# A two-layer hybrid decoder trunk on one core: the feed-forward weight buffers dealt out anew, and the scheduler's times taken from another simulation

## The chip, the core and the metric

The kernel runs on one core of a Trainium2 chip. A core has a matrix engine (TensorE, "PE" in the profile, with its weight loads as "PEld"), a vector engine (VectorE, "DVE"), an engine for activation functions and copies (ScalarE, "ACT"), a general one (GpSimd, "POOL"), and SyncE ("SP"), which here only issues DMA transfers. Each engine works through a queue of its own in order, and the queues wait for each other by semaphores. The metric is device microseconds for one execution of the program; lower is better. One execution was also taken by the hardware profiler, and its page and trace are what the prediction argues from.

## The reference

The trunk holds 16 learned meta tokens and 512 real tokens of width 1024. Layer 0 mixes by multi-scale retention (4 heads), layer 1 by a gated delta rule with a short convolution (8 heads). Behind each mixer stands a SwiGLU feed-forward block of hidden width 2816, and each of the four steps is added to the residual stream. Cut to what matters:

```python
def swiglu(h, w_gate, w_up, w_down):
    return (jax.nn.silu(h @ w_gate) * (h @ w_up)) @ w_down

for i in range(DEPTH):
    hn = rmsnorm(h, mix_norm_w[i])
    mix = retention(hn, ...) if i == 0 else gated_deltanet(hn, ...)
    h = h + mix
    h = h + swiglu(rmsnorm(h, ffn_norm_w[i]), ffn_w_gate[i], ffn_w_up[i], ffn_w_down[i])
return rmsnorm(h, final_norm_w)[:, CHUNK:, :]
```

All is float32. The kernel gets that accuracy by splitting each operand into a high and a low part in a reduced format and adding three products (`mm3`, line 400): high x high, high x low and low x high.

## The kernel before, in words

Tokens lie along the columns (528 = 16 + 512), features along the 128 partitions in 8 blocks. The stages follow each other: retention (`retention`), its output projection, feed-forward block 0 (`ffn0`), DeltaNet (`deltanet`), feed-forward block 1 (`ffn1`).

**Weights.** Every weight tile is 128 x 1024 float32 (512 KB). SyncE loads it into a raw buffer. ScalarE casts it to the high part `whi`, VectorE subtracts to get the low part `wlo` (`split_w` and `split`, line 396; in `load_w`, line 159, the same two steps are lines 170 and 171). `whi` and `wlo` have three buffers each. The raw buffers `wraw` are four, shared by the whole kernel (`raw_w`, line 174, with `RAW = 4`).

**Feed-forward, first half** (`ffn_hidden`). The 22 blocks of hidden features are worked off as 11 *quads*: a quad is two rows of blocks for gate and up, in two halves of the features, so four weight tiles called 11, 21, 22 and 12. `ffn_quad` (line 334) loads them in that order, one DMA each on SyncE's queue (line 339). The first two quads are multiplied plainly. The other nine go through `strassen` (line 342), a scheme with seven products instead of eight. Its seven products read, in order: tile 11; 21 + 22 (line 374); that plus 11 (line 377); that plus 12 (line 380); 11 + 21 (line 385, written over tile 21); tile 12; tile 22. The running sum is the one buffer `wsum`. Each product is split like a weight tile and takes 24 matmuls on TensorE (8 weight blocks of 128 x 128, three partial products each). The hidden activations leave PSUM through lines 364 and 368 and go through the SiLU and the product (lines 955 to 961).

Of a quad's four tiles, 11 and 12 stand in `wraw`, and 21 and 22 in a tag `sraw` with two buffers, in a pool that lives only as long as the first half of a block. After the first half, the down projection loads its weights into `wraw` by `load_w` (line 164 issues).

**Retention.** Its projections use a like scheme of seven products (`quad`, line 275), fed by `wraw` alone (line 257 issues, `quad_part` adds at line 264). As each product ends, `taken` copies or adds PSUM away (lines 287 to 304); line 291 is the copy after the first product, line 293 that after the second. The target of these copies is `at`, the memory that the rotary step (`rope`, line 520, VectorE operations of line 530 and splits) uses as scratch for the head before. PSUM pairs `g` are two, single banks `m` four.

**DeltaNet.** After keys, gates and values, a scan over four chunks for each head runs as a chain of small matmuls and evacuations (`dn_scan`); the projections of the following heads are interleaved with it on TensorE by hand: generators with fixed delays in "ticks", one tick for every group of matmuls (`spawn`, `tick`, and the constants `HOP`, `VALUES`, `ATTEND` and others).

**What sets the order.** The program is written in one order, which is the priority. When the `TileContext` closes, a scheduler plays the program on a simulated machine. At each simulated moment an engine takes, of the instructions whose inputs and buffers are ready there, the one that stands first in the program. The order that comes out is the order of that engine's queue on the chip, fixed from then on. Buffers of a tag are handed out in the same play: an instruction that needs a buffer becomes ready when an earlier holder has given it back.

Of the kernel before, what the change touches and what calls it, by code (L numbers as in the profile page):

```python
# [14 lines left out]
P = 128  # L15
# [35 lines left out]
class Hybrid:  # L51
# [282 lines left out]
    def ffn_quad(self, src, sp):  # L334

        raw = {}
        for i, n in enumerate(("11", "21", "22", "12")):
            raw[n] = self.raw_w() if n[0] == "1" else self.t(sp, [P, 1024], "sraw", bufs=2)
            self.nc.sync.dma_start(raw[n], src[i])
        return raw  # L340

# [1433 lines left out]
```

## Time and profile before

| | us |
|---|---|
| three runs | 1739.11, 1740.63, 1741.30 |
| median | 1740.63 |
| profiled execution: time | 1740.59 |
| profiled execution: span from first to last instruction | 1738.8 |
| mean granted TensorE clock in it | 0.990 |

How to read the profile: "busy" is the time in which an engine had an instruction in work. TensorE's matmuls are pipelined, so the durations of neighbours overlap and their starts give the pace. A wait is the idle time of an engine in front of an instruction, with the instruction that released it. The chain of waits goes back from the last instruction to what released each step. "PEclk" is the clock that TensorE was granted, as a share of full speed. A line such as L398 can be that of a helper, so the tile's name tells which use it is: `wlo<-wsum` is the low part of a running sum.

By stretches of the span, retention lies at about 10 to 372 us, its output projection at 372 to 463, feed-forward block 0 at 463 to 834, DeltaNet at 834 to 1395, and feed-forward block 1 from there to the end.

### The profile page before, as it was taken

To read this page: it belongs to the slowest core of one execution; us is meant where nothing else is said; L and a number is where in the kernel's file an instruction comes from. 1 tells how busy PE (TensorE), PEld (TensorE's weight loads), DVE (VectorE), ACT (ScalarE), POOL (GpSimd) and SP (SyncE) were. 2 spreads that over 40 slices of the span, in tenths; PEclk is the share of its full clock that TensorE was granted. 3 is DMA by queue.
4 is the path that set the end of the run, shared out by engine and by line. 5 is a ranking of instruction groups with operands and counts; after the bars stand their busy time and mean duration, and the time that the engine had idled before them with its cause. 6 is when DMAs were issued, how large, how long until landed. Compare 5 with 4: busy or idle time off the path is not lost.

```text
span 1738.8 us, 30404 instructions
## 1 busy us (share of the span) xinstructions
PE 1696.0 (98%) x12455; PEld 1577.0 (91%) x12455; DVE 1209.5 (70%) x1830; ACT 854.8 (49%) x1524; POOL 75.8 (4%) x130
## 2 busy tenths in 40 slices
PE   9999999899999999999999999999999999999997
PEld 9998989899999999999999978797977889999886
DVE  7868787873497777533688777685858797777322
ACT  5554454553354544422565537665656544445322
POOL 1000000000000000000030000010101000000010
PEclk9999999999999999999999999999999999999999
DMA  6333234472313332333264463332322233333321
GB/s 215 134 97 121 86 108 142 139 246 87 110 62 98 113 107 82 100 89 95 81 209 159 132 180 114 120 113 98 113 96 75 86 97 97 98 99 108 97 97 49
DMA packets 84524, 197.72 MB, mean 114 GB/s; under 512 B 19888, under 2 KB 37472, under 8 KB 83104
## 3 DMA queue, kind: packets, MB, share of 16 engines
q1 hardware_dynamic: 77056, 193.13, 34.2%
q10 hardware_dynamic: 6960, 1.84, 0.5%
q8 instruction: 98, 1.61, 0.4%
q0 software_dynamic: 368, 0.80, 0.1%
q14 instruction: 42, 0.34, 0.1%
HBM read 171.41 MB, written 24.33 MB: 113 GB/s over the span
## 4 chain that ended last, share of the span: by engine, by line
PE 72%; DVE 16%; ACT 5%; DMA 4%; issue 3%; POOL 1%; ACTq 0%; SPq 0%; DVEq 0%; POOLq 0%
PE g L407 53%; PE m L407 13%; DVE wlo L398 5%; ACT whi L397 3%; DMA sraw<-in_w_gu_dram 3%; DVE wraw L264 1%; DVE wsum L380 1%; DVE wsum L377 1%; DVE wsum L374 1%; DMA wraw<-in_w_ret_dram 1%; DVE xlo L530 1%; DVE wlo L171 1%; DVE xhi L398 1%; POOL ss L1435 0%; DMA xhi<-d_sg 0%
## 5 line engine op out<-in xcount | busy, mean ns | idle before, releaser
L171 DVE TENSOR_TENSOR wlo<-wraw,whi 128x1024 fp32r<-128x1024 f32 (+1 forms) x140 | 166.4, 1191 | 177.5 <-ACT whi L170 175.4
L170 ACT CAST whi<-wraw 128x1024 fp32r<-128x1024 f32 (+1 forms) x140 | 143.3, 1024 | 261.8 <-PE g L407 141.3
L407 PE MATMUL g<-fht,whi 128*128 128x264 f32 (+1 forms) x864 | 248.2, 287 | 13.2 <-ACT xlo L291 13.0
L407 PE MATMUL g<-xhi,whi 128*128 128x264 f32 (+1 forms) x1024 | 254.3, 313 | 0.1
L407 PE MATMUL g<-xhi,wlo 128*128 128x264 f32 (+1 forms) x1024 | 247.6, 306 | 2.0 <-DVE wlo L171 2.0
L407 PE MATMUL g<-xlo,whi 128*128 128x264 f32 (+1 forms) x1024 | 247.8, 306 | 0.3 <-DVE xlo L461 0.3
L407 PE MATMUL g<-fht,wlo 128*128 128x264 f32 (+1 forms) x864 | 245.6, 284 | 0.9 <-DVE wlo L398 0.8
L407 PE MATMUL g<-flt,whi 128*128 128x264 f32 (+1 forms) x864 | 245.3, 284 | 0.0
L407 PEld LDWEIGHTS g<-fht,whi 128*128 128x128 f32 x864 | 163.0, 189 | 14.0 <-ACT xlo L291 13.6
L407 PEld LDWEIGHTS g<-xhi,whi 128*128 128x128 f32 x1024 | 165.9, 189 | 10.7 <-issue 0.7
L407 PEld LDWEIGHTS g<-xhi,wlo 128*128 128x128 f32 x1024 | 165.9, 189 | 10.6 <-DVE wlo L171 2.2
L407 PEld LDWEIGHTS g<-xlo,whi 128*128 128x128 f32 x1024 | 166.2, 189 | 7.5 <-DVE xlo L461 0.7
L407 PEld LDWEIGHTS g<-fht,wlo 128*128 128x128 f32 x864 | 162.7, 188 | 1.7 <-DVE wlo L398 1.6
L407 PEld LDWEIGHTS g<-flt,whi 128*128 128x128 f32 x864 | 163.2, 189 | 0.0
L397 ACT CAST whi<-wraw 128x1024 fp32r<-128x1024 f32 x107 | 111.9, 1049 | 97.7 <-issue 36.6
L398 DVE TENSOR_TENSOR wlo<-wraw,whi 128x1024 fp32r<-128x1024 f32 x107 | 129.9, 1220 | 25.8 <-ACT whi L397 25.7
L407 PE MATMUL g<-fhb,wlo 128*128 128x264 f32 (+1 forms) x432 | 124.1, 287 | 4.8 <-DVE wlo L398 4.7
L407 PE MATMUL g<-fhb,whi 128*128 128x264 f32 (+1 forms) x432 | 123.2, 285 | 0.0
L407 PE MATMUL g<-flb,whi 128*128 128x264 f32 (+1 forms) x432 | 122.4, 283 | 0.0
L397 ACT CAST whi<-wsum 128x1024 fp32r<-128x1024 f32 x54 | 56.7, 1050 | 79.8 <-DVE wsum L377 46.7
L398 DVE TENSOR_TENSOR wlo<-wsum,whi 128x1024 fp32r<-128x1024 f32 x54 | 66.0, 1222 | 40.4 <-ACT whi L397 40.4
L407 PEld LDWEIGHTS g<-fhb,wlo 128*128 128x128 f32 x432 | 81.2, 188 | 7.5 <-DVE wlo L398 7.4
(454 smaller groups left out, 3955.6 us busy)
## 6 DMA issues: line engine op xcount, KB each, us to landing
wraw<-in_w_ret_dram SPq DMA_DIRECT2D x56, 512.0 KB, 3.4
wraw<-in_w_gu_dram SPq DMA_DIRECT2D x44, 512.0 KB, 3.4
sraw<-in_w_gu_dram SPq DMA_DIRECT2D x44, 512.0 KB, 3.4
wraw<-in_w_d_dram SPq DMA_DIRECT2D x38, 512.0 KB, 3.5
wraw<-in_w_ro_dram SPq DMA_DIRECT2D x16, 512.0 KB, 3.9
wraw<-in_w_dqk_dram SPq DMA_DIRECT2D x16, 512.0 KB, 3.3
wraw<-in_w_dv_dram SPq DMA_DIRECT2D x16, 512.0 KB, 3.6
wraw<-in_w_dg_dram SPq DMA_DIRECT2D x16, 512.0 KB, 3.4
```

The lines of the kernel that those rows point to most:

```text
L170: nc.scalar.copy(hi[:, c], raw[:, c])
L171: nc.vector.tensor_tensor(lo[:, c], raw[:, c], hi[:, c].bitcast(F32), op=ALU.subtract)
L264: self.nc.vector.tensor_tensor(raw[dst], raw[dst], raw[src], op=ALU.add)
L374: nc.vector.tensor_tensor(s, raw["21"], raw["22"], op=ALU.add)
L377: nc.vector.tensor_tensor(s, s, raw["11"], op=ALU.add)
L380: nc.vector.tensor_tensor(s, s, raw["12"], op=ALU.add)
L397: self.nc.scalar.copy(hi, src)
L398: self.nc.vector.tensor_tensor(lo, src, hi.bitcast(F32), op=ALU.subtract)
L407: mm(o, l, r[which], start=first and n == 0, stop=last and n == 2, **kw)
L530: nc.vector.tensor_tensor(o, x, y, op=op)
```

## The change

Two edits. In `ffn_quad` only tile 22 is left in `sraw`; tile 21 joins 11 and 12 in `wraw`. The numbers of buffers stay (four `wraw`, two `sraw`), and so do the loads and their order in the program. And the `TileContext` gets a flag: the scheduler plays the program on another simulated machine, a timeline simulation of the devices, in place of the one that it uses by default. The instructions of the kernel stay the same; the order of each engine's queue may differ anywhere in the program.

```diff
@@ -335,7 +335,7 @@ def ffn_quad
         raw = {}
         for i, n in enumerate(("11", "21", "22", "12")):
-            raw[n] = self.raw_w() if n[0] == "1" else self.t(sp, [P, 1024], "sraw", bufs=2)
+            raw[n] = self.t(sp, [P, 1024], "sraw", bufs=2) if n == "22" else self.raw_w()
             self.nc.sync.dma_start(raw[n], src[i])
         return raw
@@ -1768,7 +1768,7 @@ def kernel
-    with _tile.TileContext(nc) as tc:
+    with _tile.TileContext(nc, schedule_with_timeline_sim=True) as tc:
         hybrid_kernel(tc, args, out)
```

## The prediction, made before the changed kernel was run

> **What bounds the kernel now.** I read the head of the page first, then the list of who waited for whom on TensorE, then the chain of waits, and last the timelines at the places that these named.
>
> ```profile
> span 1738.8 us, 30404 instructions
> PE 1696.0 (98%) x12455; PEld 1577.0 (91%) x12455; DVE 1209.5 (70%) x1830; ACT 854.8 (49%) x1524; POOL 75.8 (4%) x130
> ```
>
> TensorE is busy for 1696.0 of 1738.8 us, and the change touches none of its work. What can be won is the idle rest, 1738.8 - 1696.0 = 42.8 us, and any time at a low clock. What can be lost has no such bound. The waits of the whole span are these (the columns are the sum in us, how many, and the longest):
>
> ```profile
> PE g L407 <- ACT xlo L291: 13.0, 3, 5.1
> PE g L407 <- DVE wlo L398: 5.5, 13, 0.6
> PE g L407 <- DVE wlo L171: 2.3, 2, 2.0
> PE m L1140 <- DVE vs L1133: 2.2, 1, 2.2
> PE m L407 <- ACT rh L397: 2.2, 5, 1.0
> ...
> PE m L1448 <- ACT vs L1436: 1.6, 3, 1.0
> PE g L407 <- ACT oh L397: 1.3, 1, 1.3
> ```
>
> Row one is retention, row two the feed-forward quads, the others DeltaNet. About 9.4 us more are idle in the last stretch, which ends in the final scaling and the stores and which nothing in this change shortens:
>
> ```profile
> 1668.00:1739.00 71.00, 61.57 (x264) 49.17 (x262) 18.12 (x25) 16.26 (x25) 6.33 (x7) 0.95 0.20 67
> ```
>
> (The columns of such a row: stretch, length, busy us of TensorE, its weight loads, VectorE, ScalarE and GpSimd, then the granted clock, the DMA share and GB/s.)
>
> **Part one, the feed-forward buffers.** Before, tiles 11 and 12 of a quad come from the four wraw buffers, and 21 and 22 from the two sraw buffers. So tile 22 of the next quad may not be fetched before the last product of this quad has had its weights split. The chain of waits shows what this does in the second feed-forward layer (start, length, what):
>
> ```profile
> 1470.38 4.33 DMA sraw<-in_w_gu_dram
> ...
> 1474.74 1.23 DVE wsum L374
> ...
> 1479.23 1.14 DVE wsum L377
> ...
> 1485.19 1.24 DVE wlo L398
> ...
> 1486.47 2.79 PE g L407 x21
> ...
> 1491.62 3.72 DMA sraw<-in_w_gu_dram
> ```
>
> The split of tile 22 ends, the load of the next one starts at 1470.38, the sum 21+22 (L374) waits for it until 1474.74, three rounds of add, cast and subtract follow, and TensorE gets the weights of the fourth product late, at 1486.47. The next load starts at 1491.62, so this quad lasts 21.24 us. The pace of TensorE alone is read in a long stretch of the same layer, 14.50 us for 119 matmuls or 0.122 us each; a quad has 7 x 24 = 168 matmuls, so 20.5 us:
>
> ```profile
> 1432.77 14.50 PE g L407 x119
> ```
>
> The loop through the DMA is thus longer than the work, by 0.7 us in this quad. The two layers differ:
>
> ```profile
> 505.00:650.00 145.00, 143.97 (x1174) 143.16 (x1173) 115.77 (x133) 71.14 (x97) 0.00 (x0) 1.00 0.31 95
> 1450.00:1600.00 150.00, 146.97 (x1207) 145.09 (x1206) 117.94 (x139) 72.81 (x103) 0.00 (x0) 1.00 0.31 96
> ```
>
> In about seven quads each, layer 0 (where a half is 264 columns wide) idles 1.0 us and layer 1 (256 columns) 3.0 us. The clock is 1.00 in both, so an idle microsecond costs no more than itself.
>
> After the change 11, 21 and 12 take wraw buffers and 22 alone takes sraw, two deep. Next quad's 11 goes into the fourth wraw buffer, next 21 into that of 11, which is free after the sum of L377 and the one of L385, both in the first half of a quad, and next 22 into the sraw buffer that the quad before gave back. The sum of L377 runs at 1479.23 in the rows above, the load of tile 22 now at 1491.62: next 21 and 22 can be issued from there on, for 22 half a quad or some 11 us earlier than now. Next 12 has the latest release, that of 21 after its split for the fifth product, and is needed only for the fourth product's sum, five products on. A load takes 4.33 us in the row above, so it is covered. The loop is cut, and what is late next is TensorE itself. This is worth the second row of the waits, **5.5 us**; bounds 0 (another wait of the same length stands behind it) and 6.4 us (0.71 us a quad in all nine of layer 1, the mean of six loops between the first and the last of the loads below, (1574.83 - 1449.63) / 6 = 20.87, against 168 x 0.120 = 20.16 by the fastest stretch of this layer). I take 5.5, the row of TensorE itself.
>
> ```profile
> 1429.89 2.88 PE m L407 x24
> ...
> 1449.63 3.76 DMA sraw<-in_w_gu_dram
> ...
> 1574.83 4.39 DMA sraw<-in_w_gu_dram
> ```
>
> The number of loads stays: per layer eleven quads of four. All stay on SyncE's queue in the order 11, 21, 22, 12. A load that waits for a wraw buffer holds up those behind it, and at the end of a layer these are the first down-projection weights:
>
> ```profile
> 669.25 0.33 SPq L164 DMA_DIRECT2D wraw<-in_w_d_dram  x1
> ...
> 681.60 17.56 SPq L164 DMA_DIRECT2D wraw<-in_w_d_dram  x4
> ```
>
> ```profile
> 693.50 1.05 ACT L170 CAST whi<-wraw 128x1024 fp32r<-128x1024 f32 x1
> ```
>
> With three buffers taken by the last quad instead of two, these two move back one release each: the load now at 669.25 becomes the first, the second takes the place of 681.60. The first of them is cast at 693.50, the second some 3 us later, so a load of 4.3 us from 681.60 still fits behind the last quad's products; I put it at nothing, and at 4.3 us at most were that cover gone.
>
> **Part two, the order.** The scheduler emits each engine's instructions as its own simulated machine finds them ready; the flag swaps that machine. No instruction is added or removed, but every queue may come out in another order, and no row of before can show it. I bound it by what order costs now. The worst place is in retention, three times alike (ScalarE, then VectorE, then TensorE; start, length, instruction, idle before and its releaser):
>
> ```profile
> 147.68 1.07 ACT L397 CAST qkhi<-xlo 128x1056 fp32r<-128x1056 f32 x1 [4.89 <-DVE xlo L530]
> ...
> 151.15 0.60 ACT L291 COPY xlo<-g 128x528 f32<-128x528 f32 x1
> ...
> 217.11 1.07 ACT L397 CAST qkhi<-xlo 128x1056 fp32r<-128x1056 f32 x1 [4.89 <-DVE xlo L530]
> ```
>
> ```profile
> 145.22 1.25 DVE L530 TENSOR_TENSOR h<-h,sinr 128x1056 f32<-128x1056 f32 x1
> 146.39 1.25 DVE L530 TENSOR_TENSOR xlo<-xlo 128x1056 f32<-128x1056 f32 x1
> ...
> 148.73 1.22 DVE L264 TENSOR_TENSOR wraw<-wraw,wraw 128x1024 f32<-128x1024 f32 x1
> 149.86 1.25 DVE L398 TENSOR_TENSOR qklo<-xlo,qkhi 128x1056 fp32r<-128x1056 f32 x1
> ```
>
> ```profile
> 151.80 0.59 PE L407 MATMUL g<-fht,whi 128*128 128x264 f32 x1 [3.94 <-ACT xlo L291]
> ```
>
> The copy L291 empties a PSUM tile into the memory that the rotary step uses as scratch, so it must wait for the last reader of that scratch, the subtraction that ends at 151.1. Two VectorE steps stand ahead of that without need: the product of 145.22 (1.17 us until the next start) and the add L264 of 148.73 (1.13 us). A better order gains at most 2.3 us of the 3.94 here, 6.9 us over the three places. Behind the waits the clock is low:
>
> ```profile
> 151.80:160.00 8.20, 8.20 (x31) 6.55 (x32) 5.96 (x10) 3.69 (x4) 0.00 (x0) 0.62 0.11 42
> 221.20:228.00 6.80, 6.76 (x24) 5.30 (x25) 5.10 (x10) 3.10 (x4) 0.00 (x0) 0.62 0.15 56
> 310.80:317.00 6.20, 6.18 (x24) 4.88 (x25) 5.96 (x10) 3.06 (x3) 0.00 (x0) 0.65 0.35 102
> ```
>
> That is 8.20 x 0.38 + 6.80 x 0.38 + 6.20 x 0.35 = 7.9 us, lost on top. Whether a wait cut to 1.6 us would still be followed by it, this row bears on:
>
> ```profile
> 874.56 1.74 PE L1140 MATMUL m<-tri,vs 128*128 128x128 f32 x8 [2.24 <-DVE vs L1133]
> ```
>
> ```profile
> 876.00:878.00 2.00, 2.00 (x11) 1.92 (x10) 1.93 (x3) 0.24 (x2) 0.01 (x1) 0.50 0.64 245
> ```
>
> A wait of only 2.24 us stands just ahead of half clock. The Trainium skill, page "TensorE: Matmul & The Clock Gate", section "Part 1", says that the clock falls to half after at least one idle window of about 3.4 us; by that rule a wait of 1.6 us costs no clock, and this term would reach 14.8 us. The row of 2.24 us speaks against so long a window here.
>
> So the term of order lies between 0 and 6.9 + 7.9 = 14.8 us of gain in retention. Likewise the DeltaNet rows of the waits sum to 2.3 + 2.2 + 2.2 + 1.6 + 1.3 = 9.6 us, the most that order can win there; what it can lose there is the slower rival. I take a third of the retention bound, **4.9 us** (near the row of the wait itself: most of it is a true dependency, and only its VectorE share depends on order), and 0 for DeltaNet, between its 9.6 us and a loss.
>
> Sum: 5.5 + 4.9 = 10.4 us. The profiled execution took 1740.6 us, its span 1738.8 and 1.8 around it, and the median of the runs is the same, 1740.6. Forecast: 1740.6 - 10.4 = **1730.2 us**. Its own range goes from 1740.6 - 5.5 - 14.8 = 1720.3 to 1735.1.
>
> **The rivals.** *The order gains nothing*: the new times rank the instructions as the old did at these places. For it: L291 waits on a real dependency, and the cast ahead of it waits 4.89 us in two of the three places, to the hundredth, so it follows from rules more than from chance. Only the buffers count: 1740.6 - 5.5 = 1735.1 us.
>
> *Given back*: the buffers gain 5.5 us and the new order makes one more wait like that of L291, 3.94 us and 7.9 / 3 = 2.6 us of clock: 1740.6 - 5.5 + 6.5 = 1741.6 us, no change that a measurement can tell.
>
> *Slower: weight casts in front of the DeltaNet scan.* The scan is a serial chain between TensorE and ScalarE, and in the same stage ScalarE casts weights ahead of need (columns: line, engine, shape, count, busy us and mean ns, idle and releaser):
>
> ```profile
> L170 ACT CAST whi<-wraw 128x1024 fp32r<-128x1024 f32 (+1 forms) x140 | 143.3, 1024 | 261.8 <-PE g L407 141.3
> ```
>
> If the new machine finds these casts ready earlier than the evacuations of the scan, each scan step waits for one cast, 1.02 us. A head has four chunks with four ScalarE steps each in its chain; for the last pair no other products are left to fill TensorE, so 16 x 1.02 = 16.4 us show, with two spells of low clock at 2.6 us: 21.6 us, less 5.5. 1740.6 + 16.1 = 1756.7 us. It decides from 6 such casts on (6.1 us against 5.5). For it: the delays in the program that spread this stage are fixed numbers, suited to one order. Against it: scan waits are now only 2.2 and 1.6 us in sum, and VectorE and ScalarE have slack.
>
> **Chances.** Forecast, both parts gain: 0.36. Order gains nothing: 0.20. Given back: 0.15. Slower: 0.29. A measurement of this kernel can tell about 0.2%, 3.5 us, from no change; the first two lie beyond it, so faster 0.56, same 0.15, slower 0.29. The range takes in the rivals on both sides: below, nearly the sum of all gains, 1740.6 - 5.5 - 14.8 - 6 (most of DeltaNet's 9.6) = 1714; above, the slower rival and two more spells of low clock, 1756.7 + 5.2, so 1762.
>
> **What would show it.** Right: no wait of TensorE on L398 in the quads and quads of layer 1 of 20.2 to 20.5 us; the sum L374 no longer waits for a DMA; the waits on L291 under 3 us, with VectorE running the subtraction of the rotary step ahead of the second product. Wrong: L291 at 13 us or more in sum with the quads free (first rival), a wait in a place that has none now (second), or TensorE idle by over 15 us between 870 and 1345 us with casts of L170 ahead of scan evacuations on ScalarE (third). The whole is wrong if the quads still wait: then something other than tile 22's buffer holds the loop.

## The result, and the profile after

| | before | after |
|---|---|---|
| median, us | 1740.97 (4 runs, 1739.11 to 1743.44) | 1797.82 (4 runs, 1793.6 to 1799.72) |
| ratio | | 1.0322, 95% interval 1.030 to 1.0345 |
| profiled execution, us | 1740.59 | 1793.6 |
| its span, us | 1738.8 | 1791.8 |
| mean granted clock | 0.990 | 0.970 |

The change makes the kernel 3.2% slower. The forecast was 1730.2 us, its range ended at 1762. The head of the page after:

```profile
span 1791.8 us, 30421 instructions
PE 1726.1 (96%) x12455; PEld 1604.1 (90%) x12455; DVE 1211.3 (68%) x1830; ACT 858.8 (48%) x1526; POOL 70.4 (4%) x130
```

TensorE runs the same 12455 matmuls; ScalarE has two instructions more, table loads of 1.28 us each (11 against 9), which came with the new order. TensorE's idle time rose from 42.8 to 1791.8 - 1726.1 = 65.7 us, by 22.9. Its busy time rose by 30.1 us, and the same matmuls are busy for longer where the clock is lower: of the 53.0 us more, over half is not waiting but slow work (a row below shows a matmul of 0.28 us that takes 0.41). These are TensorE's waits after (sum, times, longest):

```profile
PE g L407 <- ACT whi L397: 24.9, 5, 9.0
PE m L1412 <- DVE wl L398: 4.6, 7, 1.4
PE m L1448 <- ACT vs L1436: 3.3, 6, 0.9
PE m L407 <- DVE s L1423: 2.9, 7, 0.5
PE m L407 <- DVE rr L1397: 2.8, 6, 0.7
PE m L407 <- ACT rh L397: 1.9, 5, 0.7
PE g L407 <- DVE wlo L398: 1.5, 2, 1.0
```

The 13 waits of the quads on L398 are gone; two remain at the entries of the blocks. The chain of waits shows the quads of layer 1: two pieces of one kind start 20.16 us apart, and the window beside them has no idle time in 160 us:

```profile
1512.55 14.40 PE g L407 x120
...
1532.71 14.40 PE g L407 x120
```

```profile
1500.00:1660.00 160.00, 160.00 (x1325) 159.50 (x1324) 127.24 (x151) 82.80 (x114) 0.00 (x0) 1.00 0.31 103
```

So the buffers do what was expected. The first row of the waits is in part retention's old stalls, now 4.2, 4.2 and 5.8 us (13.0 us in sum before), and in part a new wait of 9.0 us at the entry of the second feed-forward block. Most of the rows below it are new or larger, many and short: they lie in DeltaNet's scan. Its four pairs of heads, from merge to merge and to the end of the scan, first before, then after:

```profile
1043.00:1105.00 62.00, 59.15 (x488) 51.45 (x487) 49.28 (x100) 45.86 (x119) 7.44 (x14) 1.00 0.35 114
1105.00:1191.00 86.00, 85.80 (x615) 71.77 (x614) 60.43 (x110) 54.86 (x127) 5.86 (x14) 1.00 0.35 113
1191.00:1277.00 86.00, 85.58 (x614) 71.76 (x614) 60.04 (x109) 54.11 (x125) 5.70 (x12) 1.00 0.33 105
1277.00:1342.00 65.00, 62.62 (x396) 47.70 (x396) 41.73 (x83) 39.86 (x97) 4.54 (x8) 1.00 0.27 91
```

```profile
1044.00:1122.00 78.00, 70.82 (x482) 57.41 (x481) 49.95 (x98) 47.10 (x119) 5.21 (x14) 0.87 0.29 95
1122.00:1217.00 95.00, 91.09 (x614) 75.95 (x614) 59.81 (x110) 53.41 (x125) 5.78 (x14) 0.95 0.30 96
1217.00:1320.00 103.00, 97.53 (x673) 82.29 (x674) 63.22 (x113) 56.55 (x131) 5.00 (x12) 0.98 0.31 99
1320.00:1387.00 67.00, 59.89 (x318) 45.41 (x312) 38.37 (x78) 36.61 (x91) 4.37 (x8) 0.82 0.19 64
```

Read the columns for length, TensorE's busy time with its matmuls, and the clock: before, 1.00 in every pair; after, 0.82 to 0.98, and the first pair takes 16 us longer for about as many matmuls.

What differs, the timeline of TensorE shows. In the same steps of a pair's chain (L1320, L1376, L1385), before:

```profile
1116.63 0.68 PE L1320 MATMUL m<-z,rr 64*64 64x64 f32 x8
...
1118.84 0.60 PE L1376 MATMUL m<-vs,um 16*16 16x256 f32 x2
...
1120.28 0.60 PE L1376 MATMUL m<-vs,um 16*16 16x256 f32 x2
```

and after:

```profile
1133.80 1.14 PE L1320 MATMUL m<-z,rr 64*64 64x64 f32 x16
1134.88 0.60 PE L1376 MATMUL m<-vs,um 16*16 16x256 f32 x2
...
1139.82 0.60 PE L1376 MATMUL m<-vs,um 16*16 16x256 f32 x2
```

The lines left out are output products of other heads (`g<-oh,whi` and the like), the filler that keeps TensorE at work while the chain goes through ScalarE and VectorE. Before, a step gets some 1 to 2 us of it; after, 4 to 5 us stand between the two steps L1376. The queue as the program has it, for the last pair (a number in brackets is filler in us at the full clock, an estimate from the columns of its matmuls; S, R, W and Wk are the matmuls of the scan on its state, its rows and its weights):

```
before: [1.4] L1314 [0.7] L1314 [1.4] L1320 [0.7] L1320 [1.4] L1376 ... [1.4] L1385 [0.7] S [0.9] S [0.5] S [0.9] S [0.5] R [0.7] R L1412 [0.9] L1412 [0.5] Wk [0.7] W Wk ...
after:  [4.5] L1314 [4.7] L1320 L1376 L1380 [3.8] L1376 [0.7] L1380 [0.5] L1385 [4.0] L1385 [0.9] S [0.2] S [3.3] S R S R L1412 R Wk L1412 W Wk S Wk S W S R S R ...
```

The filler is spent early, in bunches, and a step behind a bunch cannot start before it, since the queue is in order. Then the rest of the scan runs bare. In that part the clock falls; the same matmul in the last pair (TensorE, start, length, in brackets the wait):

```profile
1351.26 0.28 PE L407 MATMUL m<-rh,zl 128*128 128x256 f32 x1
1351.38 0.28 PE L407 MATMUL m<-rl,zh 128*128 128x256 f32 x1
1352.29 0.38 PE L407 MATMUL m<-sh,zh 128*128 128x256 f32 x1 [0.64 <-DVE rr L1397]
...
1353.76 0.33 PE L1412 MATMUL m<-ident,z 128*128 128x128 f32 x1 [0.52 <-DVE wl L398]
...
1357.32 0.41 PE L407 MATMUL m<-sh,zh 128*128 128x256 f32 x1
1357.53 0.41 PE L407 MATMUL m<-sh,zl 128*128 128x256 f32 x1
```

```profile
1355.00:1372.00 17.00, 14.87 (x56) 12.14 (x56) 12.81 (x33) 10.36 (x28) 1.53 (x3) 0.50 0.06 25
```

A matmul follows the one before by 0.12 us at 1351 and by 0.21 us at 1357: two waits of 0.64 and 0.52 us stand between, and then 17 us at half clock, in which TensorE is busy for 14.87. All this is what the two edits did together; what caused it is the matter of the runs.

### The profile page after: what moved, and what is told of

Read it like the earlier page. It is cut to its first block, busy times and chain, and to the rows that moved or that the text cites. A ratio compares the mean times of both kernels' runs of the same rounds, so it can differ in the third digit from the quotient of the medians.

```text
span 1791.8 us, 30421 instructions
## 1 busy us (share of the span) xinstructions
PE 1726.1 (96%) x12455; PEld 1604.1 (90%) x12455; DVE 1211.3 (68%) x1830; ACT 858.8 (48%) x1526; POOL 70.4 (4%) x130
## 4 chain that ended last, share of the span: by engine, by line
PE 87%; DVE 5%; ACT 3%; issue 2%; DMA 2%; POOL 1%; SPq 0%; POOLq 0%; ACTq 0%; DVEq 0%
PE g L407 66%; PE m L407 16%; DMA wraw<-in_w_ret_dram 1%; PE m L504 0%; DVE xlo L530 0%; DMA d_dec<-zl 0%; DVE h L530 0%; DMA z<-d_mp 0%; PE m L618 0%; DVE wlo L171 0%; POOL ss L1435 0%; PE m L491 0%; DVE wlo L398 0%; DMA d_m<-z 0%; PE m L1171 0%
## 5 line engine op out<-in xcount | busy, mean ns | idle before, releaser
L170 ACT CAST whi<-wraw 128x1024 fp32r<-128x1024 f32 (+1 forms) x140 | 143.4, 1025 | 326.6 <-PE g L407 205.5
L407 PE MATMUL g<-xhi,whi 128*128 128x264 f32 (+1 forms) x1024 | 250.4, 308 | 1.2 <-DVE ra L937 0.8
L397 ACT CAST whi<-wraw 128x1024 fp32r<-128x1024 f32 x129 | 134.9, 1051 | 126.1 <-PE g L407 68.3
L398 DVE TENSOR_TENSOR wlo<-wraw,whi 128x1024 fp32r<-128x1024 f32 x129 | 157.2, 1221 | 38.5 <-ACT whi L397 38.0
L407 PE MATMUL g<-fhb,whi 128*128 128x264 f32 (+1 forms) x432 | 124.1, 287 | 14.2 <-ACT whi L397 14.2
L407 PEld LDWEIGHTS g<-fhb,whi 128*128 128x128 f32 x432 | 81.9, 190 | 14.9 <-ACT whi L397 14.8
L398 DVE TENSOR_TENSOR wlo<-wsum,whi 128x1024 fp32r<-128x1024 f32 x54 | 66.2, 1225 | 40.8 <-ACT whi L397 40.8
L407 PEld LDWEIGHTS g<-flb,whi 128*128 128x128 f32 x432 | 81.6, 189 | 0.0
```

Of the source, the lines that this page charges most:

```text
L170: nc.scalar.copy(hi[:, c], raw[:, c])
L397: self.nc.scalar.copy(hi, src)
L398: self.nc.vector.tensor_tensor(lo, src, hi.bitcast(F32), op=ALU.subtract)
L407: mm(o, l, r[which], start=first and n == 0, stop=last and n == 2, **kw)
```

## The experiments

Every kernel was timed in three rounds beside the kernel before, whose medians in the four sets were 1741.58, 1742.6, 1740.84 and 1740.13 us. In the tables a profiled span is cut at two marks: the end of DeltaNet's first convolution pad (L1017), and the end of its last output product taken up (L1510).

| kernel | span | to DeltaNet | DeltaNet | rest |
|---|---|---|---|---|
| before | 1738.8 | 841.7 | 526.5 | 370.6 |
| after | 1791.8 | 843.9 | 572.7 | 375.2 |
| e1_buffers | 1728.4 | 836.9 | 526.5 | 365.0 |
| e2_flag | 1799.7 | 848.7 | 568.8 | 382.2 |

**One edit each.** The buffers alone, with the scheduler's first machine:

```diff
-    with _tile.TileContext(nc, schedule_with_timeline_sim=True) as tc:
+    with _tile.TileContext(nc) as tc:
```

> Only the weight buffers are dealt anew; the scheduler keeps its default machine. If the buffers are worth the waits of TensorE on L398 and nothing else, 1740.6 - 5.5 = 1735 us, and the nine quads of the second feed-forward layer last 20.2 to 20.5 us each. The rival, that the buffers themselves are part of the loss, expects more than 1744 us.

1732.98 us, ratio 0.9956 (0.9939 to 0.9972): 8.6 us faster. And the flag alone, with the buffers as before:

```diff
-            raw[n] = self.t(sp, [P, 1024], "sraw", bufs=2) if n == "22" else self.raw_w()
+            raw[n] = self.raw_w() if n[0] == "1" else self.t(sp, [P, 1024], "sraw", bufs=2)
```

> Only the scheduler's machine is swapped; the buffers stay as before. If the two edits add up, 1797.8 + 5.5 = 1803 us, with the quads of the second feed-forward layer still at 20.9 us. If the loss came from the two together, less than 1765 us.

1801.57 us, ratio 1.0349 (1.0334 to 1.0365). So the whole loss is the new order. Against e1_buffers the kernel after loses 63.4 us of span: 7.0 ahead of DeltaNet, 46.2 in it and 10.2 behind it. Of the 46.2 us in DeltaNet, TensorE is busy for 30.0 (515.7 to 545.7) and idle for 16.2.

**TensorE's queue held.** An order can be tried by itself: a first program is planned with one machine, its queue is read, and in the second program each instruction of that queue is tied to the one ahead of it. The other queues are planned anew by the second machine, around the one that is held, so they too come out in an order that differs from the kernel after. "In DeltaNet" is the code from the start of the scan's generators up to `ffn1`. With `pinned` standing for those ties:

```diff
-    nc = program(True)
+    nc = program(True, pinned(program(False), ("PE",)))   # ties in DeltaNet only
```

> Both edits, but in DeltaNet's scan stage TensorE's queue is put into the order that the default machine gives; all other queues are as the new machine makes them around that. Theory: the new machine puts bursts of 2 to 5 us of other products between two steps of the scan on TensorE's queue, so these run out and the rest of the scan runs bare, at a low clock; then the 46 us that the stage grew by come back, about 1752 us (1748 to 1762), and the last stretch of each pair runs at clock 1.00. Rival: the order on ScalarE and VectorE (casts ahead of the scan's evacuations) holds the scan; then it stays within 10 us of 1797.8.

1774.91 us, ratio 1.0194 (1.0179 to 1.021): 23 us back, between the two expectations. TensorE's waits show what took the place (e3, the two rows of DeltaNet that lead):

```profile
PE m L407 <- DVE rr L1397: 7.6, 10, 1.1
PE m L1290 <- DMA z<-d_mp: 7.1, 2, 3.6
```

TensorE's old queue now stands beside a new order of loads and of VectorE's work, and waits for both. So the theory that TensorE's bunches are all of it fell, and the next four runs divide the rest. First, the DMA queue held as well, ("PE", "SP"):

> Both edits, with TensorE's queue and the queue of the DMAs that SyncE issues held in DeltaNet in the order that the scheduler's first machine gives them. With TensorE's queue alone held, 1774.9 us came out, and its profile shows TensorE waiting 7.1 us for the load of z from d_mp (L1290) between 1040 and 1060 us, with the clock at 0.5 to 0.67 up to 1070 us. Theory A, that what was left there is the DMAs' order against TensorE's: those two waits go, and the 16 us that this kernel lost to the first kernel between the first and the second pair's merge (78.4 us instead of 61.9) go with them: 1759 us (1754 to 1764). Rival B, that what was left comes from the order on VectorE and ScalarE: within 5 us of 1774.9.

1768.33 us, ratio 1.0154 (1.0132 to 1.0175). The wait on z shrank to 4.4 us in one piece, and 6.6 us came back, not 16; the ten waits on L1397 stayed at 7.6 us. Both theories have a share here. Then all five queues held, in DeltaNet:

> Both edits, with the queues of all five engines held in DeltaNet in the order of the first machine, the DMAs' among them; retention, the first feed-forward block and the last block keep the new order. Theory A, that the loss in DeltaNet is a matter of queue order and nothing else: the stage takes what it takes with the buffers alone (first merge to the last output product 325 us), and only the 7 to 8 us before it and the up to 10 us at the entry of the last block are left over 1733 us: 1750 us (1741 to 1756). Rival B, that the order of the queues explains only TensorE's share and the rest comes with the new order from the stages before (transfers and clock): over 1760 us.

1744.6 us, ratio 1.0015 (1.0003 to 1.0028). DeltaNet takes 525.8 us as with the first machine: the loss there is a matter of queue order and of nothing else. Then everything held but TensorE, ("SP", "Activation", "DVE", "Pool"):

> Both edits, with the queues of SyncE's DMAs, ScalarE, VectorE and GpSimd held in DeltaNet in the order of the first machine, and TensorE's queue left to the new one. Theory A, that the bunching of filler products on TensorE's queue is the root: TensorE's queue still has bunches of 2 to 5 us between steps and bare runs of steps, so that little comes back: 1785 to 1800 us. Rival B, that the order on VectorE and ScalarE holds the steps back, and TensorE only follows: 1775 us or less.

1813.63 us, ratio 1.0412 (1.039 to 1.0434): nothing came back, and 16 us went on top, more than either expectation. And the converse, buffers new, first machine, and TensorE's queue alone in the new machine's order:

```diff
+    nc = program(False, pinned(program(True), ("PE",)))   # ties in DeltaNet only
```

> The buffers new and the scheduler's first machine, with TensorE's queue alone held in DeltaNet in the order that the new machine gives it, bunches and bare runs of steps among them. Theory A, that this order of TensorE's queue costs what it costs wherever it stands: 1733.0 us and 25 to 45 us on it, 1758 to 1778 us, with the granted clock of 1000 to 1400 us well under 1. Rival B, that it costs only together with the other queues' new order: under 1745 us.

1792.7 us, ratio 1.0289 (1.0269 to 1.0309): on a kernel of 1733.0 us TensorE's order, with the rest planned around it, costs 60 us, more than expected. The window of its last pair has the same mark as after, low clock with few idle microseconds (e8):

```profile
1327.00:1399.00 72.00, 65.41 (x338) 50.49 (x334) 41.08 (x83) 38.84 (x98) 4.97 (x8) 0.74 0.17 59
```

The lengths of DeltaNet beside each other:

| TensorE's queue | the others | DeltaNet, us | run |
|---|---|---|---|
| old | old | 526.5; 525.8 | e1; e6 |
| old | planned by the second machine around it | 553.4 | e3 |
| old | DMAs old, the rest planned by the second machine around both | 549.5 | e5 |
| new | new | 572.7 | after |
| planned by the second machine around the others | old | 593.4 | e7 |
| new | planned by the first machine around it | 587.7 | e8 |

The traces show which orders these are. By line, tile and shape, the last 2400 matmuls of DeltaNet follow each other in e8 as in the kernel after, and in e3 and e6 as in e1. In e7 TensorE's queue parts from the kernel after at the 85th matmul from the end: it is a third order, and e7 does not price the new one.

TensorE's new order is thus enough for the loss: with the rest planned around it by the first machine it costs 61 us, where the whole loss in DeltaNet is 46 (e8). It is not all of it in the kernel after: with TensorE's old queue 19 of the 46 us came back, and the other queues as the second machine plans them around it cost 27 (e3). The costs do not add up; that the queues of one plan fit each other would explain it. That it is the bunches in TensorE's new order that cost the time is read off its timeline; no run moved the filler and left the rest of that order alone.

**The entry of the last block.** Behind DeltaNet the kernels after and e6 lose 9 to 10 us. In e6 TensorE's wait there is much the same as after (9.0 us there):

```profile
PE g L407 <- ACT whi L397: 8.5, 1, 8.5
```

The timeline of ScalarE in the kernel after says where it begins: the row factor `rb` of the norm waits 4.54 us for TensorE's small matmul L500, which stands behind other matmuls in the queue.

```profile
1433.88 0.17 ACT L508 COPY rb<-m 128x16 f32<-128x16 f32 x1 [4.54 <-PE m L500]
```

So all queues were held from DeltaNet to the end of the program:

> Both edits, with the queues of all five engines held in the first machine's order from DeltaNet to the end of the program; only retention and the first feed-forward block keep the new order. Theory A, that the wait of 8.5 us at the entry of the last block is a matter of order too (the steps of its row norm stand behind other products in TensorE's queue): the 9 to 10 us there go as well, and what stays over 1733 us is the 6 us lost before DeltaNet: 1735 to 1740 us against 1744.6 with DeltaNet alone held. Rival B, that this wait comes from the time at which DeltaNet ends or from the transfers: within 3 us of 1744.6.

1736.33 us, ratio 0.9976 (0.9965 to 0.9986): the rest takes 365.0 us as in e1_buffers, so this wait is order too; that it begins with L500 is read off the timeline. Of 63.4 us some 8 us ahead of DeltaNet are left (845.2 us to the mark against 836.9); no run held the queues there.

**Retention's three stalls.** The prediction's gain by order sat here. First the scratch that it named, taken away from the rotation, on e1_buffers:

```diff
-            return self.spawn(self.rope(qk, ct, at, cosr, sinr), ROPED)
+            return self.spawn(self.rope(qk, ct, bt, cosr, sinr), ROPED)
```

> The buffers dealt anew, the default machine, and the rotary step of heads 1 to 3 takes the other half of the scratch memory (bt in place of at), so that the copy after the first product of the next quad (L291) no longer waits for the rotary step. If that copy waits for the scratch and not for a place in ScalarE's queue, the 13.0 us of waits and 7.9 us of low clock go: 1735.1 - 20.9 = 1714 us. If ScalarE's in-order queue holds it (the cast of the rotary result stands ahead of it and waits for VectorE), it gains under 7 us: 1728 to 1735 us.

1730.39 us, ratio 0.994 (0.9925 to 0.9954): 2.6 us under e1_buffers, with runs of the two that overlap. The number is that of the second expectation, but its reason is not what the trace shows. The copy L291 is free of the scratch, and TensorE still waits 3.27, 3.27 and 3.31 us, now for weights. VectorE's timeline has the reason (the first place and the instructions ahead of it):

```profile
146.33 1.25 DVE L530 TENSOR_TENSOR xlo<-xlo 128x1056 f32<-128x1056 f32 x1
147.50 1.25 DVE L530 TENSOR_TENSOR h<-h,cosr 128x1056 f32<-128x1056 f32 x1
148.67 1.22 DVE L264 TENSOR_TENSOR wraw<-wraw,wraw 128x1024 f32<-128x1024 f32 x1
149.80 1.25 DVE L398 TENSOR_TENSOR qklo<-xlo,qkhi 128x1056 fp32r<-128x1056 f32 x1
```

```profile
151.07 0.59 PE L407 MATMUL g<-fht,whi 128*128 128x264 f32 x1 [3.27 <-ACT whi L397]
```

Each starts as the one before ends, back to 139.4 us: rotation, weight sums, splits. If VectorE is full, work must leave it. The 2.35 us of scaling a stored head (L781), then also one multiplication of the rotation, went to GpSimd (cut to the calls; the two helpers get the engine as an argument):

```diff
-            normed(orow)
+            normed(orow, nc.gpsimd)
             nc.sync.dma_start(d_o[hd], oraw)
```

> The kernel with the buffers alone and the scratch of its own for the rotation, and the scaling of a stored head (L781, 2.35 us on VectorE just ahead of each rotation) on GpSimd. Theory A, that retention's three stalls (9.8 us in the scratch kernel, 3.3 us each) are VectorE's queue with no gap from 139 to 156 us, weight sums, splits and rotation in one line: 2.3 us less on VectorE ahead of each of them takes as much from each, 5 to 7 us in all: 1723 to 1726 us against 1730.4. Rival B, that the rotation's own chain between ScalarE and VectorE sets the end of the stall: 1729 us or more, the three waits still about 3.3 us each.

```diff
-        tt(t2, t2, cos)
+        tt(t2, t2, cos, eng=nc.gpsimd)
```

> As the kernel before in this list, and one of the rotation's multiplications (t2 by cos, 1.17 us on VectorE) on GpSimd as well. Theory A: 1.2 us less again at each of the three places, 3.5 us of 3.3 us stalls in all, so that they all but go: 1719 to 1723 us. Rival B, that the rotation's chain sets the end: no gain over the kernel before, and a loss of up to 2 us a place where the slower GpSimd multiplication lands late: 1729 to 1736 us.

1733.37 us (0.9961, 0.9947 to 0.9975) and 1745.04 us (1.0033, 1.0018 to 1.0047). The first is a number of rival B, the second lies above even that, and the reason is another, as the last section shows. So the scaling was left out altogether:

```diff
-            normed(orow)
             nc.sync.dma_start(d_o[hd], oraw)
```

> The kernel with the buffers alone and the scratch of its own for the rotation (1730.4 us), and the scaling of the three stored heads (L781, 2.35 us each on VectorE) left out altogether: that part of the computation is missing. Theory A, that retention's three stalls are VectorE's full queue: 2.35 us less on VectorE ahead of a stall shortens it by as much, and nothing stands on GpSimd in VectorE's way: 4 to 7 us, 1723 to 1726 us. Rival B, that the stalls are set by the rotation's own chain: 1729 us or more.

1717.98 us, ratio 0.987 (0.985 to 0.989): 12.4 us under e4_scratch, for 3 x 2.35 us = 7.05 us taken from VectorE. Rival B falls, and theory A's cause holds, but not its sum: the three waits are 1.71, 1.71 and 2.98 us, 3.4 us less together, and 8.4 us of the gain is busy time of TensorE (1692.5 to 1684.1), since the clock stays up at all three (the first place in e4, then in e11, then the third in e11):

```profile
140.00:175.00 35.00, 30.86 (x217) 28.88 (x217) 30.22 (x41) 14.02 (x20) 0.00 (x0) 0.90 0.32 103
```

```profile
149.45 0.39 PE L407 MATMUL g<-fht,wlo 128*128 128x264 f32 x1 [1.71 <-DVE wlo L398]
```

```profile
140.00:175.00 35.00, 33.29 (x261) 32.16 (x260) 32.65 (x47) 16.41 (x23) 0.00 (x0) 1.00 0.28 91
```

```profile
299.07 0.39 PE L407 MATMUL g<-fht,wlo 128*128 128x264 f32 x1 [2.98 <-DVE wlo L398]
```

```profile
290.00:330.00 40.00, 36.30 (x284) 34.96 (x283) 37.38 (x53) 20.29 (x30) 0.00 (x0) 1.00 0.38 132
```

What is left in e11 is a matter of place in VectorE's queue. ScalarE has cast these weights by 143.40 us, and VectorE's split of them starts at 148.18, behind four more steps of the rotation (ScalarE, then VectorE):

```profile
142.35 1.05 ACT L397 CAST whi<-wraw 128x1024 fp32r<-128x1024 f32 x1
```

```profile
148.18 1.22 DVE L398 TENSOR_TENSOR wlo<-wraw,whi 128x1024 fp32r<-128x1024 f32 x1
```

Whether that split put first would gain, or only move the wait to the rotated head that TensorE needs next, no run shows.

Of the complete kernels, e4_scratch at 1730.4 us and e1_buffers at 1733.0 us are the fastest; e9_norm_gpsimd at 1733.4 us is level with the latter. The first machine's order with the new buffers is the version to keep.

## Why the prediction was wrong, point by point

*What bounds the kernel.* Right: TensorE, and "what can be lost has no such bound" was to the point. The range did not follow from it.

*The feed-forward buffers, 5.5 us.* Right in mechanism and a little small: 8.6 us by e1_buffers. The waits on L398 went, TensorE's idle time fell by 42.8 - (1728.4 - 1691.1) = 5.5 us to the digit, and quads of layer 1 take 20.16 us, below the stated 20.2 to 20.5. TensorE's busy time fell by 4.9 us besides, so idle time alone undercounted the gain; what of that is clock was not followed up. Beside the flag the buffers are worth less, 3.7 us (1801.57 against 1797.82).

*The order, 4.9 us of gain.* This is the step that failed. It was "a third of the retention bound", with "0 for DeltaNet". In retention the order gained nothing (14.2 us of waits against 13.0). The wait was read as that of the copy L291, whose releaser came last; with the copy freed of the scratch, 3.27 of the 3.94 us at the first place stayed, as a wait for weights out of the same VectorE queue (e4), and less work in that queue shortened it (e11). The bound of 2.3 us a place priced a wait behind which another of nearly the same length stood. That no order of VectorE's steps would gain here is not shown, since no run moved one. In DeltaNet the order lost 46.2 us, and 17 us at the entries and before. A gain was read from rows of the stage with the largest single wait, while the loss came where before had almost none. The absence of waits in the scan was the product of the old order, which dealt filler of about 1 us to each step, and no reserve.

*Rival 1, order gains nothing,* was right for retention alone. *Rival 2, given back,* had the kind, one new wait (9.0 us at the last block's entry, where it priced 3.94), but not the extent.

*Rival 3, slower.* Its place, DeltaNet, was right, and half of its sign came: TensorE is idle for 17.9 us between 870 and 1345 us (10.5 before). That the last pair has no filler left was wrong for the kernel before, where the listing above has filler from step to step; it became so in the new order. Its mechanism was not what happened: in the four pairs 16 of ScalarE's instructions of the scan start as a cast of L170 ends, against 24 before. TensorE's own queue is enough for the loss (e8), with filler in bunches ahead of chain steps. And its price, 21.6 us, counted one late step at a time. It allowed two spells of low clock at 2.6 us, where the clock was low over much of the four pairs: 30.1 us more busy time in all, the largest term left out.

*The clock.* The row of 2.24 us before half clock was taken as evidence against the Trainium skill's window of about 3.4 us (page "TensorE: Matmul & The Clock Gate", section "Part 1"); the bound of 14.8 us stayed, and a third of it was taken for another reason, that most of the wait is a true dependency. In retention the traces come nearer to the page's rule: with waits of 1.71 and of 2.98 us the clock stayed at 1.00 (e11), with 3.27 us it fell to 0.90 over 35 us (e4). In DeltaNet they do not: half clock followed the single wait of 2.24 us before, and waits of 0.64 and 0.52 us in the scan after. So the length of one wait does not tell it here. The same page's section "A second HAM failure mode: psum-queue depth-cycling" says of another kernel that frequent small pauses between groups of matmuls make the clock swing. The trace is of that kind: in the 4 us ahead of 1355 TensorE was idle 1.24 us, and no wait in the scan was longer than 1.4 us.

*Chances.* Slower had 0.29, and the range ended at its one mechanism. An edit that can reorder every queue of a kernel 98% busy on one engine should have had a far wider upper end.

What stays open: why the new machine deals filler out in bunches (that it reckons the steps of the chain as later than they are is an inference from the order), how much of TensorE's share is the bunches, and the 7 to 8 us ahead of DeltaNet, part of which is waits of 0.8, 1.6 and 1.0 us at the entry of the first feed-forward block.

## What to carry to other kernels

A planner's order is a set of queues that fit each other: to find what a new order costs, hold one queue at a time and then all, in both directions. A queue that is not held is planned anew, so look which order it got, and do not expect the shares to add up. Where a serial chain is covered by filler on an in-order queue, look at how the filler is dealt out, not only whether there is enough: here bunches of 4 to 5 us went with a chain whose end ran bare and at half clock. And when an engine works without a gap ahead of a stall, see whether its work can be shortened, and do not take the last releaser for the only one: behind it another may stand.

## What the runs showed of the hardware that was not expected

**GpSimd stops VectorE.** With the scaling on GpSimd (e9), VectorE's two weight sums of some 1.2 us each take 6.90 us; the rows are VectorE's, then GpSimd's:

```profile
134.43 6.90 DVE L264 TENSOR_TENSOR wraw<-wraw,wraw 128x1024 f32<-128x1024 f32 x2 [0.44 <-DMA wraw<-in_w_ret_dram]
```

```profile
135.34 4.90 POOL L781 TENSOR_TENSOR h<-h,rb 128x2112 f32<-128x2112 f32 x1 [0.48 <-ACT rb L509]
```

In e10 the rotation's subtraction takes 3.50 us instead of 1.25 while GpSimd multiplies for 3.34:

```profile
150.89 3.50 DVE L530 TENSOR_TENSOR xlo<-xlo 128x1056 f32<-128x1056 f32 x1
```

```profile
149.94 3.34 POOL L530 TENSOR_TENSOR h<-h,cosr 128x1056 f32<-128x1056 f32 x1 [8.38 <-DVE xlo L530]
```

The work moved off VectorE thus comes back as VectorE's standstill, at about twice its length (some 4.5 us for 2.35 us moved, and 2.25 for 1.25). The Trainium skill, page "SBUF — State Buffer", section "Who interferes with whom", says that a VectorE instruction with two inputs in SBUF and a GpSimd instruction that reads SBUF exclude each other for the whole instruction; these rows agree.

**A small cut of a wait can give back more than its length.** In retention 7.05 us less work on VectorE gave 12.4 us: the waits shrank by 3.4 us in sum, and the clock, 0.97 from 100 to 420 us in e4, was 1.00 there in e11. The third wait shrank by only 0.33 us, from 3.31 to 2.98, and its half clock went all the same.
